# A written order for in-projection, attention and both feed-forward products of a Strassen-Winograd transformer layer

## The chip, the cores and the metric

The kernel runs on one core of one Trainium2 chip. What counts is the device time of one execution in microseconds, as the median of several runs. A profile is one execution taken by the hardware profiler. A core has five engines that run their own queues of instructions: TensorE (PE, with its weight loads shown as PEld), VectorE (DVE), ScalarE (ACT), GpSimd (POOL) and SyncE (SP). SP, ACT and POOL also issue DMA transfers.

## The reference, cut to what matters

One layer, S = 512 tokens, D = 2048, DFF = 8192, eight attention heads of 128, all in float32:

```python
h = rmsnorm(x, g_mix[l])
z = jnp.einsum('bsd,dc->bsc', h, w_in[l])
cb, cc, cv, q, k, v, f_logit, gate_c, gate_a = jnp.split(z, SPLIT_POINTS, axis=-1)
conv_branch = jnp.einsum('bsc,cd->bsd', cb * causal_dwconv(cc * cv, conv_w[l]), w_conv_out[l])
log_f = jax.nn.log_sigmoid(f_logit + b_f[l])
attn = forgetting_attention(q, k, v, log_f)     # softmax(q k / sqrt(d) + c_q - c_k, causal) v, c = cumsum(log_f)
attn_branch = jnp.einsum('bsc,cd->bsd', attn, w_attn_out[l])
mixed = sigmoid(gate_c + b_c) * conv_branch + sigmoid(gate_a + b_a) * attn_branch
x = x + jnp.einsum('bsd,de->bse', mixed, w_mix_out[l])
h2 = rmsnorm(x, g_mlp[l])
u = jnp.square(jnp.maximum(jnp.einsum('bsd,df->bsf', h2, w_ff1[l]), 0.0))
x = x + jnp.einsum('bsf,fd->bsd', u, w_ff2[l])
return rmsnorm(x, g_final)
```

The lines are shortened; the gates, the merge and the squared ReLU are written as one line each.

## The kernel before, in words

**Products.** The in-projection, ff1 and ff2 are cut into 2 x 2 blocks, and each such block product is done by Strassen-Winograd with seven products instead of eight. They are named by their operand on the side of the tokens: A11, A12, A22 and the sums S1 to S4. On the side of the weights stand four quarters X00, X01, X10 and X11, each of 1 MB, 128 x 2048, and sums of them that DVE makes in place (`sub`, L104). Before TensorE can use a quarter it is split: ACT copies it to a rounded high half (`th`, L100), DVE subtracts that to get the low half (`tl`, L101). A product is then three passes, high by high, high by low and low by high. In the in-projection and ff1 (`mm_cols`, L142, L144, L146) a product is 48 matmuls of width 256; the low half is used only by the last 16. In the V groups and ff2 (`mm_rows`, L159, L161, L164) it is 24 matmuls of width 512 (narrower in V). `th` and `tl` have two buffers each, the quarters four (x0 to x3), and results in flight (`o`) five.

**Groups.** A `Group` holds the seven products of one set of columns. `head` runs A11 and A12, `tail` the other five in the order S4, S2, S3, S1, A22; between them stand the sums of the quarters and the evictions of the accumulators a to d, one PSUM bank each. The stages in order of time: RMSNorm and transposes of x; heads of five groups (V and four of k and q), their tails; the second V group; six groups for the conv's inputs (z) and, ahead of the first four of them in the text, the eight calls of `attend(h)`; then eight groups for the gates; the outputs of conv and attention (`gemm_t`); the mix product (`gemm_n`); sixteen groups of ff1; ff2 in eight segments of two units of seven products; the final norm and the output.

**Attention.** For each head and each block of 128 query rows, TensorE makes the scores (L547 to L549), DVE the maximum (L551), ACT the exponential (L557), DVE scales, TensorE transposes (L563), DVE copies (L565), TensorE multiplies with v (L567). k, q and v of a head come back from DRAM (kq_d, v_d) over SP's queue.

**What sets the order.** The text gives every instruction, but the framework's scheduler decides where it stands on its engine, so a piece of attention lands wherever it fits between or inside products. In z and gates, groups n = 4, 7, 10 and 13 have a matmul of width 192 into an unused bank in the middle of S4 (`apart`), and so has every third group of ff1. All loads of weights and nearly all stores and reloads of intermediate results are issued by SP. The feed-forward's sums for ff2 (`s_d`, L858 and L859) go out by POOL through one buffer `r`, and are loaded again as `us` (L908) by POOL.

**ff2.** Each unit loads four weight quarters (y, L973), runs A11, S3, S2, A22, S1, A12, S4 and adds its accumulators unscaled to the result of 128 x 1024 at a time (`into`, L107). In the last segment the row factor `turned`, the residual and the gain of the last norm are applied (`finish`, L941 and L944; `residual`).

## Time and profile before

| | us |
|---|---|
| three runs | 2488.52, 2493.36, 2494.16 (median 2493.36) |
| the profiled execution | 2488.25 |
| its span in the trace | 2486.4 |
| start of the first and of the last group of matmuls | 6.5 and 2472.2 |
| attention and its 28 products | 272 to 492 |
| rest of z, and gates | 492 to about 870 |
| ff1 | about 1230 to 1855 |
| ff2 | 1856 to 2474 |

The page gives for every engine its busy time and share of the span, then the span in slices. A row of a window gives start:end, its length, then busy time and count of instructions for each engine, the clock granted to TensorE (1.00 is full), the share of the DMA engines and the rate in GB/s. A row of waits reads: the waiting engine, what it would write, its line, an arrow, the engine and line that released it, and then total us, how often, and the longest. A row of the timeline or of the chain begins with start and duration.

### The profile page before, as it was taken

The numbers are of one execution on the slowest core, as the hardware profiler recorded it, in microseconds if no ns is written. First come the engines' busy times: TensorE is split into PE (matmuls) and PEld (weight loads), VectorE is DVE, ScalarE is ACT, GpSimd is POOL, SyncE is SP. The second block draws the span as 40 slices with busy tenths as digits, with TensorE's granted clock in tenths as the row PEclk, the third lists the DMA queues.
The fourth block names the chain that finished last, engine by engine and source line by source line (L and its number), as shares of the span: only waits on it lengthen the run. The fifth ranks groups of instructions, "written<-read, shape, count | busy, mean of one in ns | idle before, by whom it ended". The sixth has DMA issues, their size and how long they took to land.

```text
span 2486.4 us, 39025 instructions
## 1 busy us (share of the span) xinstructions
PE 2436.8 (98%) x16910; PEld 2250.5 (91%) x16910; DVE 1898.7 (76%) x1498; ACT 1146.3 (46%) x1136; POOL 112.3 (5%) x184
## 2 busy tenths in 40 slices
PE   8999999999999999999999999999999999999997
PEld 7999999999999988888889999999998888888885
DVE  7877676789777743425688898888987888878888
ACT  5433443344544622225556666656665333333344
POOL 0000000000000000000000000000011000000010
PEclk9999999999999999999999999999999999999998
DMA  7555544456544554335645656556488566655573
GB/s 239 169 168 160 156 133 149 143 172 219 161 132 132 184 167 154 115 136 200 214 160 189 231 180 225 198 197 239 173 302 295 185 217 220 236 183 175 201 254 118
DMA packets 289920, 465.08 MB, mean 187 GB/s; under 512 B 10236, under 2 KB 194644, under 8 KB 289620
## 3 DMA queue, kind: packets, MB, share of 16 engines
q1 hardware_dynamic: 260704, 330.40, 41.6%
q0 software_dynamic: 28176, 131.08, 14.1%
q8 instruction: 133, 2.18, 0.4%
q10 hardware_dynamic: 868, 1.10, 0.1%
q14 instruction: 39, 0.32, 0.0%
HBM read 370.26 MB, written 92.27 MB: 186 GB/s over the span
## 4 chain that ended last, share of the span: by engine, by line
PE 68%; DVE 8%; DMA 4%; issue 2%; ACT 2%; SPq 0%; POOL 0%; POOLq 0%; DVEq 0%; ACTq 0%
PE pn L326 7%; PE pt L307 7%; PE a L142 5%; PE a L144 5%; PE a L146 4%; PE a L159 4%; PE a L164 4%; PE a L161 4%; DVE tl L101 3%; PE d L144 3%; PE d L142 3%; PE d L146 3%; PE d L159 2%; PE d L161 2%; PE d L164 2%; DMA x<-in_w_ff_dram 2%
## 5 line engine op out<-in xcount | busy, mean ns | idle before, releaser
L101 DVE TENSOR_TENSOR tl<-x,th 128x2048 fp32r<-128x2048 f32 (+1 forms) x252 | 574.9, 2287 | 208.3 <-ACT th L100 185.9
L100 ACT ACTIVATE th<-x 128x2048 fp32r<-128x2048 f32 (+1 forms) x252 | 482.4, 1917 | 507.7 <-PE a L144 170.5
L104 DVE TENSOR_TENSOR x<-x,x 128x2048 f32<-128x2048 f32 (+1 forms) x144 | 329.1, 2285 | 18.4 <-DMA x<-in_w_ff_dram 10.9
L100 ACT ACTIVATE th<-y 128x2048 fp32r<-128x2048 f32 x80 | 153.5, 1918 | 245.7 <-DVE y L104 92.4
L101 DVE TENSOR_TENSOR tl<-y,th 128x2048 fp32r<-128x2048 f32 x80 | 182.7, 2284 | 35.2 <-ACT th L100 35.2
L142 PE MATMUL a<-ST,th 128*128 128x256 f32 x768 | 179.6, 279 | 7.1 <-ACT th L100 7.1
L101 DVE TENSOR_TENSOR tl<-raw,th 128x2048 fp32r<-128x2048 f32 x40 | 91.6, 2290 | 121.2 <-ACT th L100 121.0
L144 PE MATMUL a<-ST,th 128*128 128x256 f32 x768 | 178.7, 278 | 0.0
L100 ACT ACTIVATE th<-raw 128x2048 fp32r<-128x2048 f32 x40 | 76.8, 1920 | 210.8 <-PE pt L307 107.3
L159 PE MATMUL a<-th,us 128*128 128x512 f32 x512 | 157.7, 389 | 1.5 <-ACT o L867 1.5
L161 PE MATMUL a<-th,us 128*128 128x512 f32 x512 | 157.6, 389 | 0.0
L142 PEld LDWEIGHTS a<-ST,th 128*128 128x128 f32 x768 | 145.4, 189 | 8.2 <-ACT th L100 7.9
L144 PEld LDWEIGHTS a<-ST,th 128*128 128x128 f32 x768 | 145.3, 189 | 0.0
L142 PE MATMUL a<-S,th 128*128 128x256 f32 x576 | 133.9, 278 | 4.1 <-ACT th L100 4.1
L326 PE MATMUL pn<-th,m 128*128 128x512 f32 x512 | 134.4, 391 | 0.0
L144 PE MATMUL a<-S,th 128*128 128x256 f32 x576 | 133.4, 277 | 0.0
L307 PE MATMUL pt<-act,th 128*128 128x512 f32 x512 | 126.6, 389 | 1.0 <-DVE o L107 1.0
L164 PE MATMUL a<-tl,us 128*128 128x512 f32 x512 | 126.4, 389 | 0.0
L142 PE MATMUL d<-ST,th 128*128 128x256 f32 x512 | 118.3, 277 | 0.0
L144 PE MATMUL d<-ST,th 128*128 128x256 f32 x512 | 118.2, 277 | 0.0
L159 PEld LDWEIGHTS a<-th,us 128*128 128x128 f32 x512 | 96.0, 188 | 21.6 <-ACT o L867 1.6
L307 PEld LDWEIGHTS pt<-act,th 128*128 128x128 f32 x512 | 96.0, 188 | 21.0 <-issue 1.2
(280 smaller groups left out, 5860.0 us busy)
## 6 DMA issues: line engine op xcount, KB each, us to landing
x<-in_w_in_dram SPq DMA_DIRECT2D x86, 1024.0 KB, 5.8
x<-in_w_ff_dram SPq DMA_DIRECT2D x66, 1024.0 KB, 8.3
y<-in_w_ff_dram SPq DMA_DIRECT2D x64, 1024.0 KB, 6.3
us<-s_d POOLq DMA_DIRECT2D x48, 1024.0 KB, 8.9
s_d<-rh POOLq DMA_DIRECT2D x32, 896.0 KB, 5.9
s_d<-r POOLq DMA_DIRECT2D x32, 896.0 KB, 8.0
raw<-in_w_mix_out_dram SPq DMA_DIRECT2D x24, 1024.0 KB, 5.1
g_d<-o SPq DMA_DIRECT2D x32, 256.0 KB, 2.2
```

Of the source, the lines that this page charges most:

```text
L100: nc.scalar.activation(out=hi, in_=src, func=AF.Copy)
L101: nc.vector.tensor_tensor(out=lo, in0=src, in1=hi.bitcast(F32), op=ALU.subtract)
L104: nc.vector.tensor_tensor(out=out, in0=a, in1=b, op=ALU.subtract)
L142: nc.tensor.matmul(o, hi[:, q, js], Sh, start=first and q == 0 and j == 0, stop=False, skip_group_check=True)
L144: nc.tensor.matmul(o, hi[:, q, js], Sl, start=False, stop=False, skip_group_check=True)
L146: nc.tensor.matmul(o, lo[:, q, js], Sh, start=False, stop=q == nq - 1, skip_group_check=True)
L159: nc.tensor.matmul(o, Sh[:, ts], hi[:, q, :], start=begin, stop=False, skip_group_check=True)
L161: nc.tensor.matmul(o, Sl[:, ts], hi[:, q, :], start=False, stop=False, skip_group_check=True)
L164: nc.tensor.matmul(o, Sh[:, ts], lo[:, q, :], start=False, stop=q == nq - 1, skip_group_check=True)
L307: nc.tensor.matmul(ps[j], w[:, q, j * P:(j + 1) * P], a, start=first, stop=last)
L326: nc.tensor.matmul(ps[t], A[t][e], w[:, q, :], start=first, stop=last)
```

## The change

The tails of the first five groups and everything up to the end of the gates, and then ff1, ff2 and the end, stand in blocks in which the scheduler is switched off (`with manual()`) for TensorE, DVE, ACT, POOL and SP: their queues hold the instructions in the order of the text. The rest (start, the five heads, conv and attention outputs, mix) is scheduled as before. The text of that order is written by a `Pipe`. Its step k emits, for product k: an attention piece if one is due, a sum, the split, another sum; then the eviction of product k-2, the store of product k-3, work postponed to this step; then the matmuls of product k-1:

```diff
+    class Pipe:
+        def step(self, p=None, sub=None, after=None, early=None, guest=False):
...
+            visit = self.visits.pop(0) if guest and self.visits else None
+            if visit:
+                p.high()
+                visit.first()
+            if sub:
+                sub()
+            if p:
+                p.split()
+            if visit:
+                visit.second()
+            if after:
+                after()
+            if last and not early:
+                last.evict()
+            if old:
+                old.finish()
+            for work in self.todo.pop(self.n, ()):
+                work()
+            if cur:
+                cur.go()
...
-            self.run(c, "S4", X[1, 1], True)
-            sub(X[0, 0], X[0, 1], X[0, 0])
-            sub(X[0, 1], X[1, 1], X[0, 1])
...
+            pipe.step(self.product("S4", (1, 1), "c", True), after=next(turns), guest=True)
+            p = self.product("S3", (0, 1), "d", True)
+            pipe.step(p, after=next(turns))
+            p = self.product("S2", (0, 0), "a", False)
+            pipe.step(p, after=next(turns), guest=True)
+            p = self.product("A22", (1, 0), "d", False)
+            pipe.step(p, after=next(turns), guest=True)
+            p = self.product("S1", (1, 1), "a", False)
+            pipe.step(p, guest=True)
```

The pipe isn't emptied at the end of a group: the first products of the next group follow in the same steps, and each quarter of the next group is loaded as soon as one of this group's buffers comes free. The order within a group is now A11, A12, S4, S3, S2, A22, S1.

**Attention** is 24 pieces: per head rows 0 and 1 together, row 2, row 3. A visit stands at the start of a product, in five of the seven products of a group: TensorE does the output of the piece before last, the transposes of the last one and the scores of the new one, and then the product. With two visits for the forget sums and two to run out they fill the 28 products of the first groups of z. The convolutions stand in the first four groups of gates, and the reload and split of the conv's and attention's results in the last one. The fetch of the next head's k, q and v is issued by POOL in the visit that reads the last row of the head before:

```diff
+        def first():
+            if a:
+                a.out()
+            if b:
+                b.turned()
+            if c:
+                c.scores(i)
+            if b:
+                b.kept()
+            if c:
+                c.weigh()
+            if a and a.at[-1][0] == NT - 1:
+                a.stored()
+            if c and c.at[-1][0] == NT - 1 and i + 1 < len(rows):
+                rows[i + 1].fetch()
```

On TensorE, in the attention, stood before (th and tl are the halves of weights, S_885 a sum of tokens, o, tp and sc the attention's output, transposes and scores):

```order
L146 MATMUL a<-S_885,tl 128x256 x2
L567 MATMUL o<-pt,vv 128x128 x3
L146 MATMUL a<-S_885,tl 128x256
L563 MATMUL tp<-ident,p 128x128 x4
L146 MATMUL a<-S_885,tl 128x256 x8
L567 MATMUL o<-pt,vv 128x128 x4
L146 MATMUL a<-S_885,tl 128x256 x5
```

and stands now, at the border of two products:

```order
L150 MATMUL a<-A_146,tl 128x256 x16
L737 MATMUL o<-pt,vv 128x128 x3
L726 MATMUL tp<-ident,p 128x128 x3
L699 MATMUL sc<-kT,qT 128x512
L700 LDWEIGHTS sel
L700 MATMUL sc<-cparts,sel 128x512
L701 LDWEIGHTS identb
L701 MATMUL sc<-maskb,identb 128x128
L146 MATMUL b<-A_147,th 128x256
```

The pieces of attention have moved from inside a product to its end, three kinds together.

**Stores and fetches** of v, k and q, z, gates, attention and conv results go from SP's queue to POOL's (`nc.sync.dma_start` becomes `nc.gpsimd.dma_start`), so that SP issues in these stages the loads of weights alone. POOL's queue in the attention now reads (none of these stood there before):

```order
L690 DMA kT<-kq_d 128x512
L690 DMA qT<-kq_d 128x512
L692 DMA vv<-v_d 128x4x128
L773 DMA z_d<-o 128x2x256 x2
L690 DMA kT<-kq_d 128x512
L690 DMA qT<-kq_d 128x512
L692 DMA vv<-v_d 128x4x128
```

A fetch of a head and the stores of z share one queue here. The four dummy matmuls of z and gates are removed; those of ff1 stay.

**ff1's start.** All four quarters of the first group are loaded first. The transposes of the last columns of tokens (`Q2.turn(1, 3)`) stand inside A11's matmuls, the mean over rows comes only after S4 is issued, S4 takes the token chunks of the last column at its end (`late`), and of that column's sums the low halves of S2 and S1 are postponed:

```diff
+    with manual():
+        g0 = groups[0]
+        for ij in ((0, 0), (1, 0), (1, 1), (0, 1)):
+            g0.load(*ij)
+        g0.begin(True, True)
+        squares_of_rows()
+        Q2.gained(1, 3)
+        behind = []
+        Q2.sums(3, behind)
...
+        g0.rest(groups[1], at)
+        chain(groups[1:], units[0], lambda n: load_sums(0, LOADS.index(n)) if n in LOADS else None)
+        for unit, ahead in zip(units, units[1:]):
+            unit.run(ahead, during(unit))
+        units[-1].close()
```

**ff2.** The order of a unit is A11, A12, S2, S3, S1, A22, S4, and in the last unit A11, S3, S2, A22, S1, A12, S4, with S4's matmuls by blocks of rows, one block to its end and then the other. Each eviction is a scaled addition of 128 x 512 (`turned`, L1238) per bank, so the row factor is applied from the start; residuals are added in segments 1 to 4, the gain of the last norm four or eight steps after the last eviction. The sums of a unit's weights are made partly one unit ahead, which needs X11 of the next unit in the buffer that the S4 of this one frees. DVE before, across a change of unit (y are quarters, t a sum, x the result):

```order
L101 TENSOR_TENSOR tl<-y_19170,th 128x2048
L101 TENSOR_TENSOR tl<-y_19395,th 128x2048
L104 TENSOR_TENSOR y_19395<-y_19397,y_19395 128x2048
L104 TENSOR_TENSOR y_19397<-y_19399,y_19397 128x2048
L107 TENSOR_TENSOR x_18493<-a,x_18493 128x2x512
L104 TENSOR_TENSOR t_19462<-y_19399,y_19395 128x2048
L101 TENSOR_TENSOR tl<-y_19397,th 128x2048
```

and now, where the second row is the low half of S4 and y_19598 is the next unit's X11, loaded into the buffer of y_19365:

```order
L106 TENSOR_TENSOR t_18429<-y_19500,y_19400 128x2048
L106 TENSOR_TENSOR tl<-y_19365,th 128x2048
L1238 SCALAR_TENSOR_TENSOR x_18428<-a,turned,x_18428 128x512 x2
L106 TENSOR_TENSOR tl<-y_19400,th 128x2048
L1238 SCALAR_TENSOR_TENSOR x_18428<-d,turned,x_18428 128x512 x2
L106 TENSOR_TENSOR t_18429<-y_19598,t_18429 128x2048
L106 TENSOR_TENSOR tl<-y_19502,th 128x2048
L1238 SCALAR_TENSOR_TENSOR x_18427<-a,turned,x_18427 128x512 x2
```

Between the release of the buffer and the first reader of the new quarter stand two evictions and one low half. The loads of `us` are split by products (A11 and A12; S2 and S3; S1 and A22; S4) and issued by POOL as soon as the products of the segment before that read the same place are done. At the end, a row's output is two transfers of 512 KB, one by ACT and one by SP.

More of the change, by code (lines that the diff above doesn't have):

```diff
@@ L211, in snap, with plus @@
             return s
-        def plus(self, s, ps, scale=1.0):
+        def plus(self, s, which, scale=1.0):
+            ps = self.A[which]
             if len(ps) == 1:
@@ L639, in tile_hybrid_block, with acted @@
+    seq = heads + [gV1] + zs + gates
+    with manual():
+        for g, after in zip(seq, seq[1:] + [None]):
+            if "a" not in g.A:
+                g.begin(True)
+            g.rest(after, during(g))
+        take(2)
+        pipe.end()
+        pipe.drain()
+    def acted(*tags):
+        return lambda k: tuple(e[:, k % 4, :] for e in acts[tags[k // 4]])
+    yact, aact = acted(0, 1), acted(2, 3)
     ph.close()
```

922 lines of the change are left out of this document (557 added, 365 removed).

## The prediction

> **What bounds the kernel now.** I read the page first, for the engine that is full.
>
> ```profile
> span 2486.4 us, 39025 instructions
> PE 2436.8 (98%) x16910; PEld 2250.5 (91%) x16910; DVE 1898.7 (76%) x1498; ACT 1146.3 (46%) x1136; POOL 112.3 (5%) x184
> PE   8999999999999999999999999999999999999997
> ```
>
> TensorE is busy in 98% of the span, and the change leaves its matmuls as they are (four dummies fewer). So it can only win the time in which TensorE stands, starts cold or runs below its pace. The table of windows, asked by stage, shows where that is (columns: window, length, busy time of PE, PEld, DVE, ACT, POOL, granted clock, DMA share, GB/s).
>
> ```profile
> 75.00:245.00 170.00, 163.98 (x1417) 162.79 (x1416) 134.63 (x75) 65.91 (x48) 3.79 (x4) 1.00 0.52 164
> 272.00:492.10 220.10, 217.26 (x1726) 201.49 (x1725) 160.08 (x236) 88.85 (x122) 0.10 (x1) 1.00 0.45 142
> 1225.00:1375.00 150.00, 141.69 (x1189) 139.79 (x1187) 121.25 (x95) 83.35 (x88) 7.72 (x13) 0.99 0.54 178
> 1288.00:1298.00 10.00, 7.26 (x51) 7.06 (x50) 10.00 (x7) 6.31 (x5) 1.15 (x2) 0.83 0.45 184
> 1375.00:1850.00 475.00, 474.78 (x4172) 474.35 (x4171) 415.12 (x310) 299.94 (x299) 28.19 (x52) 1.00 0.60 212
> 1900.00:2430.00 530.00, 530.00 (x2340) 438.85 (x2339) 440.74 (x248) 193.20 (x114) 44.54 (x60) 1.00 0.64 213
> 2438.00:2444.00 6.00, 4.29 (x12) 3.45 (x13) 6.00 (x4) 3.57 (x2) 0.00 (x0) 0.72 0.01 3
> 2474.00:2486.40 12.40, 0.15 (x1) 0.00 (x0) 4.16 (x9) 4.65 (x9) 1.10 (x2) 0.62 0.87 328
> ```
>
> Steady ff1 and steady ff2 (1375 to 1850, 1900 to 2430) have nothing to win: TensorE never stops, at 113.9 ns per 256-wide matmul (475/4172) and 226.5 ns per 512-wide one. The losses are at the seams: tails of the heads, attention, the start of ff1, the last ff2 unit, the end. What TensorE waits for there, from the view of waits by window (total, times, longest):
>
> ```profile
> PE a L142 <- ACT th L100: 3.6, 4, 1.4
> PE a L159 <- ACT th L100: 1.5, 1, 1.5
> PE c L159 <- ACT th L100: 0.9, 1, 0.9
> ...
> PE sc L547 <- DMA qT<-kq_d: 2.4, 3, 1.0
> ...
> PE a L142 <- ACT th L100: 6.9, 3, 2.7
> PE c L142 <- ACT th L100: 1.4, 1, 1.4
> ...
> PE pt L307 <- DVE o L107: 1.0, 1, 1.0
> PE a L159 <- ACT o L867: 1.5, 1, 1.5
> PE d L159 <- ACT th L100: 4.6, 1, 4.6
> ```
>
> The first three are the tails (6.0 us), the fourth attention, the next two the start of ff1 (8.3 us), the last three the start of the conv output, the start of ff2 and its last unit. Nearly always the high half (th, ACT) of a product comes late, although ACT is 46% busy: it waits itself for a sum on DVE. The order of DVE's queue decides, and that is what the change rewrites.
>
> A second loss is pace. Three runs of 16 equal matmuls in the chain: in the attention stage, in the gates and at the start of ff1.
>
> ```profile
> 430.85 1.89 PE a L146 x16
> ...
> 551.14 1.81 PE a L146 x16
> ...
> 1339.39 1.88 PE a L146 x16
> ```
>
> That is 118, 113 and 118 ns, 5.67 or 5.43 us per product of 48. In the records a stretch keeps one pace for many products and changes it at an interruption; an attention piece often leaves the slow one behind.
>
> **The change part by part.** Each gain is what a stage loses now, less what I expect to stay.
>
> Attention. 28 products at 5.44 us are 152.3 us of the stage's 220.1. The prices of its pieces are distances in the timeline and one run of the chain:
>
> ```profile
> 383.44 0.38 PE L547 MATMUL sc<-kT,qT 128*128 128x128 f32 x2
> 384.40 0.36 PE L142 MATMUL a<-A,th 128*128 128x256 f32 x1
> 392.19 1.13 PE L547 MATMUL sc<-kT,qT 128*128 128x512 f32 x2
> 393.40 0.36 PE L142 MATMUL b<-A,th 128*128 128x256 f32 x1
> 425.12 1.02 PE o L567 x8
> ```
>
> Scores of two short rows together, or of row 2, take 0.96 us (384.40 - 383.44; I take the same for row 2), of row 3 1.21: 8 x 3.13 = 25.0 us. The 160 output matmuls and 80 transposes of width 128 lie between 0.113 us (a 256-wide one) and 1.02/8 = 0.127: 27 to 30.5. With 1 to 3 for the forget sums (eight small instructions, where 1.21 pays three), 53 to 58.5 us; so 9 to 15 are lost now to slow pace, restarts and waits. Afterwards a product is interrupted once, at its start, and not at several places inside. I leave 4 to 5 (slow pace after half of 28 visits 0.24 x 14 = 3.4, the fetch of qT 0 to 2): **gain 7**, bounds 0 and 12.
>
> The fetch is the new exposed step. kT and qT of the next head may be issued only when row 3's scores have read the old ones; the next scores come after one product (5.44) and about 1 us of output and transposes: some 6.5 us. Their landings before, and the issue time of a POOL transfer (longer ones, hence an upper end):
>
> ```profile
> kT<-kq_d SPq DMA_DIRECT2D x8, 256.0 KB, 6.0
> qT<-kq_d SPq DMA_DIRECT2D x8, 256.0 KB, 3.2
> L908 POOL DMA_DIRECT2D us<-s_d x64: 748/748/770, 1830.4 to 2392.6; - x64
> ```
>
> Two issues (1.5) and 3.2 to 6.0 make 4.7 to 7.5: nothing to 1 us at each head change, seven times, fewer where the visit pattern leaves two products between. That is the 0 to 2 above, at worst 7. Stores moved from SP to POOL cost TensorE nothing: they sit behind an eviction, and no matmul waits for them; gone from SP, they no longer hold up weight loads behind an SP wait.
>
> Here a page speaks against the change. Row L908: 64 issues of POOL take 748 to 770 ns while DVE is busy in 83% of the window (440.74/530), so nothing shows POOL being shut out. The Trainium skill, "DMA: Bandwidth & Descriptors", section "SWDGE vs HWDGE vs iDMA", says that descriptor rings of POOL-issued transfers are SBUF state from which DVE locks GpSimd out in its 2-port mode, and that transfers issued from SP or ACT are immune. By that rule the moved fetches would be late; it is a rival below.
>
> Tails of V and kq. 6.0 us of waits. The pipe emits the split of product k while k-1 runs, and sums one product ahead: **gain 5.5**, 0 to 6.
>
> Start of the conv output and of ff2: waits of 1.0 and 1.5. The first goes because the reload and split of y and a is spread over the last gate group, the second because ff2's first sums are loaded and split in the same pipe: **gain 1.2 each**, 0 to 1.5.
>
> Start of ff1. 8.3 us of waits, 10 us at a clock of 0.83 behind the longest (1.7), and seven products at slow pace (1.7): 11.7. The chain shows why: a weight quarter arrives late, and sums and splits queue behind it.
>
> ```profile
> 1270.74 7.88 DMA x<-in_w_ff_dram
> 1278.64 2.29 DVE x L104
> ```
>
> Afterwards all four quarters are loaded ahead, the sums of the last column are cut into two urgent and two postponed low halves, and S4 takes that column's chunks last: **gain 10**, 5 to 11.7.
>
> Last ff2 unit. A wait of 4.6, then 6 us at 0.72 (1.7): DVE is busy for the whole of that window and just before it, with finishing passes of the unit before queued ahead of this unit's sums. Afterwards the sums are made a product ahead and the gain passes are postponed by four to eight steps: **gain 5.3**, 2 to 6.3. End: 12.4 us follow the last matmul. S4 by row blocks closes one half early and each row leaves in two larger transfers; the last eviction, mean, scaling and transfer stay: **gain 2**, 0 to 4.
>
> ff2's steady state is where the change can cost. Evictions become one scaled pass per bank; DVE's prices in the chain of waits, and the landings of weight loads (y, from the source view: min, median, max):
>
> ```profile
> 2425.93 1.40 DVE x L941 x2
> 2427.33 2.20 DVE tl L101
> 2435.45 2.21 DVE y L104
> DMA to landing us min/median/max: 6.0/6.3/11.4
> ```
>
> Per unit 7 low halves and 4 sums at 2.2 and 12 evictions at 0.7: 32.6 us (33.8 with a residual, half the elements of a sum and so about 1.2) of 7 x 5.44 = 38.1. It fits, at 86 to 89%. But in written order DVE stops at whatever is late. The next unit's X11 can be loaded only into the buffer that S4's low half releases, about when TensorE ends S1. Its first reader stands behind the eviction of A22: 5.44 + 1.40 = 6.9 us later, and about 1 more passes before TensorE notices. So up to 7.9 us (6.7 with the residual) cost nothing; 6.3 is free; the high end, 11.4, is 3.5 too late. At the 7 changes of segment a pair of us loads is in flight when X11 is issued; the middle of 6.3 and 11.4, about 9, costs there (9 - 7.9) x 7 = 8, plus 1.2 for four residuals = 12 at most. I take **loss 5**, 0 to 17.
>
> Steady ff1. A chain through the single r buffer is written out too. Its DVE work is as before (415.12 of 475), it has about 2 us to spare per group, and the store's landing lies within it (row of L859):
>
> ```profile
> DMA to landing us min/median/max: 3.8/8.0/10.0
> ```
>
> **Loss 1**, 0 to 5.
>
> The sum: 7 + 5.5 + 1.2 + 1.2 + 10 + 5.3 + 2 = 32.2 gained, 6 lost, 26.2 net. The profiled execution took 2488.25 us in all, so 2462. The median of the three runs, 2493.36, lies 5.1 above that execution, which is below the lowest of them (2488.52); I add about half: **2464 us**. Gains and losses at their better ends (44 and 0) would give 2446; with attention 4, ff1's start 4 and ff2 6 worse, 2478: that is the case's own range.
>
> **Rivals.**
> *Slow pace stays* (0.22). Four dummy matmuls are gone from z and gates, where the row of 551.14 shows the fast pace. If the last visit leaves the slow pace, the rest of z and eight groups of gates, some 58 products, run at 5.67: 58 x 0.24 = 14 us, 2478. For it: the row of 430.85. Against it: the pace changes at interruptions, and the last visits (outputs and transposes without scores) and every short wait are further ones that can bring the fast one back.
>
> *DVE locks out POOL* (0.05). Each fetch of kT and qT waits for a DVE pass, up to 2.2 us each, at up to seven head changes: half of 7 x 4.4 = 15 us, 2479; row L908 speaks against it.
>
> *The X11 loop decides, and it gets slower* (0.08). If X11 lands at 11.4 us at all 15 changes of unit, 15 x 3.5 + 8 x 1.2 = 62 us are lost instead of 5: 2521. It eats the whole gain of about 31 from a mean landing near 9.5 us on ((9.5 - 7.9) x 15 + 9.6 = 34). For it: the single slot and the maximum 11.4. Against it: the median 6.3, and us loads fall on half of the changes.
>
> *The written order does not deliver in attention* (0.07). A visit's DVE work is bound to scores on TensorE:
>
> ```profile
> L565 DVE COPY pt<-tp 128x128 f32<-128x128 f32 (+3 forms) x32 | 15.7, 489 | 19.2 <-PE tp L563 19.1
> L551 DVE TENSOR_REDUCE nm<-sc 128x1 f32<-128x128 f32 (+3 forms) x32 | 15.1, 482 | 10.2 <-PE sc L549 9.7
> ```
>
> Copy 0.5, maximum 0.5 to 0.7, low half 2.2, scaling about 0.4, one sum 2.2, eviction 0.7: 6.6 of the 5.44 + 1.9 = 7.3 us of a step. If ACT's exponential in the middle costs 1.5 more, every one of 28 steps is late by 0.8: 22 us, 2486 to 2490.
>
> *All at their better ends* (0.08): 2444 to 2450.
>
> **How the numbers follow.** Forecast 0.50, slow pace 0.22, lock 0.05, X11 0.08, attention 0.07, better 0.08. Low 2445, high 2487: outside are X11, half of attention and some of the better end, about 0.15. A measurement of this kernel tells about 0.2% from no change, 5 us. Faster (under 2488.4): 0.50 + 0.22 + 0.05 + 0.08 + a part of attention = 0.87; the same 0.05; slower 0.08, the X11 case.
>
> **What would show it.** Right: no wait above 1 us at the start of ff1 nor in the last unit, granted clock 1.00 there; the time between the first and last score near 213 us instead of 220; 256-wide runs of 16 in the gates at 1.81. Wrong: gates at 1.89; waits of TensorE for th in ff2, with DVE idle until y lands, at each unit's A12 or S2; waits of sc for qT above 1 us at every head; POOL issues longer than 0.77 us. If steady ff2 needs more than 38.2 us per unit, the forecast falls by its own term.

## The result and the profile after

The changed kernel takes 2464.26 us (median of 4 runs, 2461.30 to 2467.21), the kernel before 2491.64 (4 runs, 2488.52 to 2494.16). The ratio is 0.9891, with a 95% interval of 0.9873 to 0.9908. The profiled execution of the changed kernel took 2464.56, which is 23.7 less than that of before. The forecast for it was 2462, and 2464 for the median. The median was met within 1 us, the profiled execution within 3. The stages below show that this is partly luck: the gains in attention, ff1 and the tails were forecast too low, and the loss in ff2 was forecast at about a third of what it was.

The page of the changed kernel (span; busy time by engine; TensorE and its granted clock in 40 slices):

```profile
span 2462.8 us, 39037 instructions
PE 2429.9 (99%) x16906; PEld 2243.7 (91%) x16906; DVE 1914.6 (78%) x1557; ACT 1147.0 (47%) x1140; POOL 214.7 (9%) x343
PE   7999999999999999999999999999999999999998
PEclk9999999999999999999999999999999999999999
```

TensorE now is busy in 99% of a shorter span. The last slice of the clock, an 8 in the kernel before, is a 9 now. POOL's busy time doubled, since it issues the stores and fetches.

To compare the stages I cut both traces at the same events: first product of the tails, first product of z, first matmul of the conv output, first product of ff1, first matmul of ff2, last matmul, end. The table of windows of before, cut there (the second number is a stage's length):

```profile
0.00:87.40 87.40, 74.08 (x610) 73.07 (x610) 68.57 (x80) 48.58 (x60) 7.12 (x17) 0.98 0.73 230
87.40:272.00 184.60, 179.49 (x1541) 178.50 (x1542) 138.68 (x79) 73.02 (x56) 0.00 (x0) 1.00 0.52 163
272.00:875.30 603.30, 599.00 (x5091) 582.86 (x5089) 462.83 (x440) 276.33 (x309) 0.81 (x8) 1.00 0.50 156
875.30:1230.10 354.80, 354.80 (x1593) 294.13 (x1594) 162.78 (x173) 121.27 (x158) 11.06 (x15) 1.00 0.49 165
1230.10:1858.20 628.10, 618.11 (x5394) 616.49 (x5393) 540.20 (x409) 385.87 (x391) 39.12 (x70) 1.00 0.59 206
1858.20:2473.80 615.60, 610.99 (x2688) 505.43 (x2688) 521.28 (x314) 236.38 (x157) 53.05 (x73) 1.00 0.62 208
2473.80:2486.40 12.60, 0.35 (x2) 0.00 (x0) 4.36 (x10) 4.85 (x10) 1.10 (x2) 0.63 0.87 330
```

The same of the changed kernel:

```profile
0.00:88.80 88.80, 75.52 (x610) 74.57 (x611) 68.67 (x80) 48.53 (x60) 9.73 (x21) 0.98 0.71 226
88.80:266.80 178.00, 178.00 (x1543) 178.00 (x1542) 134.70 (x75) 72.34 (x54) 13.08 (x18) 1.00 0.54 170
266.80:857.80 591.00, 590.88 (x5087) 578.55 (x5085) 463.31 (x425) 270.71 (x302) 86.21 (x143) 1.00 0.50 158
857.80:1213.10 355.30, 355.08 (x1593) 294.00 (x1593) 169.41 (x180) 125.54 (x166) 13.13 (x18) 1.00 0.50 168
1213.10:1828.20 615.10, 612.99 (x5394) 612.36 (x5394) 541.18 (x405) 386.38 (x386) 38.53 (x69) 1.00 0.59 203
1828.20:2452.50 624.30, 617.02 (x2690) 506.28 (x2689) 533.70 (x388) 240.53 (x171) 52.96 (x73) 0.99 0.62 213
2452.50:2462.80 10.30, 0.38 (x2) 0.00 (x0) 3.58 (x8) 2.97 (x5) 1.10 (x2) 0.63 0.51 205
```

The count of matmuls in a row is the same within four, so each pair of rows holds the same work. The lengths give:

| stage | before | after | won | forecast |
|---|---|---|---|---|
| start and heads | 87.4 | 88.8 | -1.4 | 0 |
| tails of V and kq, second V group | 184.6 | 178.0 | 6.6 | 5.5 |
| z with attention, gates | 603.3 | 591.0 | 12.3 | 8.2 |
| conv and attention outputs, mix | 354.8 | 355.3 | -0.5 | 0 |
| ff1 | 628.1 | 615.1 | 13.0 | 10.2 |
| ff2 | 615.6 | 624.3 | -8.7 | 0.3 |
| after the last matmul | 12.6 | 10.3 | 2.3 | 2 |
| span | 2486.4 | 2462.8 | 23.6 | 26.2 |

(The waits before the conv output and before ff2 end at the cuts, so in the forecast's column the first 1.2 stands with z, and the second with ff1, beside the 10 and the loss of 1. ff2 has the last unit's 5.3 and the loss of 5.) ff2 got slower where I had it about even. What TensorE still waits for from the tails on, in the changed kernel's view of waits:

```profile
PE a L164 <- DVE x L1238: 4.0, 1, 4.0
PE a L164 <- ACT th L245: 3.0, 2, 2.8
...
PE d L139 <- ACT th L245: 0.8, 1, 0.8
PE a L146 <- ACT o L288: 0.7, 1, 0.7
PE a L150 <- DVE tl L106: 0.6, 1, 0.6
```

The first two rows are ff2 (L164 is its first pass), the other three the start of ff1. The waits for th in the tails are gone, and so are all waits for qT. The two in ff2 also cost the clock, as the windows around them show:

```profile
1860.00:1872.00 12.00, 8.04 (x23) 5.88 (x22) 10.52 (x8) 1.40 (x1) 0.00 (x0) 0.72 0.71 234
1922.00:1930.00 8.00, 5.07 (x15) 3.49 (x15) 8.00 (x6) 1.91 (x1) 0.00 (x0) 0.79 0.46 163
```

In the first, 12 us hold 23 matmuls of 0.2265 us, or 5.2 us of work: 6.8 us are lost, 4.0 by the wait and 2.8 by the clock at 0.72. In the second 8.0 - 15 x 0.2265 = 4.6 us are lost, 2.8 of them by a wait for a high half. DVE's timeline at the first shows how it came about:

```profile
1851.61 2.28 DVE L106 TENSOR_TENSOR tl<-t,th 128x2048 fp32r<-128x2048 f32 x1
1859.95 2.29 DVE L106 TENSOR_TENSOR t<-y,y 128x2048 f32<-128x2048 f32 x1 [6.06 <-DMA y<-in_w_ff_dram]
1862.16 2.28 DVE L106 TENSOR_TENSOR tl<-y,th 128x2048 fp32r<-128x2048 f32 x1
1864.36 1.40 DVE L1238 SCALAR_TENSOR_TENSOR x<-a,turned,x 128x512 f32<-128x512 f32 x2
```

DVE stands 6.06 us before the sum for the next unit, whose quarter is late. Behind that sum in its queue lie a low half and the eviction of S1. TensorE needs the bank of S1 for S4. It had finished what precedes S4 at about 1861 and goes on at 1865.20, when the first half of the eviction is done. The sum itself wasn't urgent; the eviction was.

### The profile page after: what moved, and what is told of

The parts are those of the page before. It is cut to its first block, busy times and chain, and to the rows that moved or that the text cites. A ratio compares the mean times of both kernels' runs of the same rounds, so it can differ in the third digit from the quotient of the medians.

```text
span 2462.8 us, 39037 instructions
## 1 busy us (share of the span) xinstructions
PE 2429.9 (99%) x16906; PEld 2243.7 (91%) x16906; DVE 1914.6 (78%) x1557; ACT 1147.0 (47%) x1140; POOL 214.7 (9%) x343
## 4 chain that ended last, share of the span: by engine, by line
PE 93%; DVE 3%; issue 2%; ACT 1%; DMA 1%; POOL 0%; ACTq 0%; POOLq 0%; DVEq 0%
PE a L146 7%; PE a L148 7%; PE a L150 7%; PE pn L465 7%; PE pt L446 7%; PE a L164 5%; PE d L146 5%; PE a L166 5%; PE d L148 5%; PE d L150 5%; PE a L169 5%; PE b L146 2%; PE d L166 2%; PE d L164 2%; PE b L148 2%; PE c L146 2%
## 5 line engine op out<-in xcount | busy, mean ns | idle before, releaser
L106 DVE TENSOR_TENSOR x<-x,x 128x2048 f32<-128x2048 f32 (+1 forms) x108 | 246.8, 2286 | 2.8 <-DMA x<-in_w_ff_dram 2.7
L245 ACT ACTIVATE th<-y 128x2048 fp32r<-128x2048 f32 x66 | 126.8, 1922 | 208.6 <-PE a L166 107.0
L164 PE MATMUL a<-th,us 128*128 128x512 f32 x512 | 163.2, 397 | 7.3 <-DVE x L1238 4.0
L245 ACT ACTIVATE th<-t 128x2048 fp32r<-128x2048 f32 x46 | 88.2, 1918 | 156.2 <-PE a L166 97.0
L106 DVE TENSOR_TENSOR tl<-y,th 128x2048 fp32r<-128x2048 f32 x66 | 150.9, 2286 | 12.9 <-ACT th L245 12.9
L166 PE MATMUL a<-th,us 128*128 128x512 f32 x512 | 160.7, 394 | 0.0
L106 DVE TENSOR_TENSOR tl<-t,th 128x2048 fp32r<-128x2048 f32 x46 | 105.3, 2290 | 51.6 <-ACT th L245 51.6
L164 PEld LDWEIGHTS a<-th,us 128*128 128x128 f32 x512 | 97.6, 191 | 32.3 <-issue 4.9
L146 PE MATMUL d<-ST,th 128*128 128x256 f32 x512 | 117.8, 276 | 0.0
```

Source lines behind the costliest of these rows:

```text
L106: nc.vector.tensor_tensor(out=out, in0=a, in1=b, op=ALU.subtract)
L146: nc.tensor.matmul(o, hi[:, q, js], Sh, start=first and q == 0 and j == 0, stop=False, skip_group_check=True)
L164: nc.tensor.matmul(o, Sh[:, ts], hi[:, q, :], start=begin, stop=False, skip_group_check=True)
L166: nc.tensor.matmul(o, Sl[:, ts], hi[:, q, :], start=False, stop=False, skip_group_check=True)
L245: nc.scalar.activation(out=self.hi, in_=self.src, func=AF.Copy)
```

## The experiments

**Two losses in ff2, one edit each.** The first edit moves the broadcast of the last norm's gain (gf). In the changed kernel it is issued at the end of segment 0, and it landed late (row of its source line: min, median, max):

```profile
DMA to landing us min/median/max: 13.3/13.3/13.3
```

```diff
-        nc.gpsimd.dma_start(out=late["gf"], in_=g_final.partition_broadcast(P))
+    def fetch_gain():
+        nc.gpsimd.dma_start(out=late["gf"], in_=g_final.partition_broadcast(P))
...
+            if n == "S2" and (seg, cg) == (5, 0):
+                fetch_gain()
```

> The changed kernel with one edit: the broadcast of the last norm's gain (gf) is issued in segment 5 and not at the end of segment 0. Theory A, a transfer in the way: gf (13.3 us to land) delays X11 of the third ff2 unit, which landed after 12.1 us; without it X11 lands in 6 to 9 us, the 3.0 us wait of TensorE at about 1922 and the 2 us of cold clock behind it go, and the profiled execution falls from 2464.6 to about 2460. Rival B, the pairs of us loads alone delay X11: it still takes 10 us or more, the wait stays, 2464.

Measured: 2457.99 us (one run, span 2456.3). ff2 took 619.0 us from its first to its last matmul, and not 624.3. X11 of the third unit landed after 6.39 us instead of 12.1, and from 1900 to 2400 TensorE ran without a stop, 499.90 us of 500 for 2201 matmuls. Theory A holds for the second loss: the broadcast was in the way. In segment 5 gf itself took 12.6 us, and nobody waited for it.

The second edit evicts S1 first in the first unit:

```diff
                       self.minus(u[:, 1], ahead.X[0, 1], ahead.X[0, 0]),
+                      early=(lambda p: None) if self.u is None else None)
```

> The changed kernel with one edit: in the first ff2 unit alone DVE evicts S1 before, not after, the sum for the next unit and the low half of S4. Theory A, an in-order queue: DVE stood 6.1 us before a sum whose quarter was late, and the eviction for which TensorE waited was queued behind it; with the eviction ahead, the wait of 4.0 us at about 1861 and 3.2 us of cold clock go, 2464.6 to about 2457.5. Rival B, the late quarter itself is needed: the low half of S4 then comes late in its place, 2 to 4 us of wait stay, 2460 to 2463.

Measured: 2464.22 us (one run), no change. The view of waits, 1850 to 1935, tells why:

```profile
PE a L164 <- DVE x L1238: 4.8, 1, 4.8
PE a L164 <- ACT th L245: 2.3, 1, 2.3
PE a L166 <- DMA us<-s_d: 1.4, 1, 1.4
```

The first wait did go. 1.4 us remained of it, now for the loads of us. But a wait of 4.8 us for an eviction now stands at 1900, at the S4 of the second unit, with a cold clock behind it. The same queue order is in every unit, and the quarter that the second unit's sum reads came late too: it landed after 15.0 us. Neither theory had it: the gain was given back one unit later, because the fault was in the rule and the edit mended one place of it.

Both edits:

```diff
+    def fetch_gain():
...
+                      early=(lambda p: None) if self.u is None else None)
```

> Both edits together, gf in segment 5 and S1 evicted first in the first unit. Theory A: the two losses are separate and add, 12 us, about 2452.5 profiled; ratio to the kernel before about 0.984. Rival B: removing the first stall brings TensorE earlier to the second, and only the larger one is won, 2457 to 2460.

Measured: median 2462.27 (4 runs, 2459.55 to 2465.96), ratio 0.9876 (0.9855 to 0.9897). Theory A was wrong, and B's value was too good: the second unit's wait stayed (5.0 us for the eviction), so of the two gains only that of gf is there (ff2 620.8 us), and the interval doesn't tell it from the changed kernel.

The next variant asks for X11 earlier, by putting the sum behind the low half of S4:

```diff
             pipe.step(self.product("S4", X[1, 1], "a", False, (0, 1, True)),
-                      self.minus(u[:, 1], ahead.X[0, 1], ahead.X[0, 0]),
+                      after=self.minus(u[:, 1], ahead.X[0, 1], ahead.X[0, 0]),
                       early=(lambda p: None) if self.u is None else None)
```

> As e3, and in every unit the sum X01 - X00 of the next unit stands behind the low half of S4 instead of ahead of it, so that X11 of the next unit is asked for one DVE pass (2.2 us) earlier. If the X11 loop has its slack in the steady state (my sum: a landing up to 7.9 us is free, and 6.1 to 6.3 was measured there), the time is that of e3 within 1 us, and only DVE's waits for y shrink (22.8 us in 12 places). If the loop is at its limit, 2 to 5 us are won over e3.

Measured: median 2463.98 (4 runs), ratio 0.9880 (0.9864 to 0.9897). DVE's waits for y fell from 22.8 to 3.0 us, and the time didn't fall. No long wait is left in ff2, but the units from the second to the fourteenth lose 0.65 to 0.71 us each at S4 (38.73 to 38.79 us a unit; the kernel before takes 38.08). Rows of DVE and of TensorE around one of them:

```profile
1935.31 2.29 DVE L106 TENSOR_TENSOR tl<-y,th 128x2048 fp32r<-128x2048 f32 x1 [0.70 <-ACT th L245]
1937.52 2.29 DVE L106 TENSOR_TENSOR t<-y,y 128x2048 f32<-128x2048 f32 x1
1939.72 1.40 DVE L1240 SCALAR_TENSOR_TENSOR x<-a,turned,x 128x512 f32<-128x512 f32 x2
```

```profile
1940.56 1.11 PE L164 MATMUL a<-th,us 128*128 128x512 f32 x2
1941.51 0.62 PE L166 MATMUL a<-th,us 128*128 128x512 f32 x2
```

The eviction of S1 starts at 1939.72 and takes 0.7 us per bank. TensorE could have begun S4 a little earlier and follows it bank by bank. Here the low half starts only when ACT's high half is there, and the eviction still comes last. So the eviction is what must not stand behind the sum. Hence the version that mends the rule, with gf in segment 5 and in each unit low half, eviction, sum:

```diff
             if last and not early:
                 last.evict()
+            if behind:
+                behind()
...
             pipe.step(self.product("S4", X[1, 1], "a", False, (0, 1, True)),
-                      self.minus(u[:, 1], ahead.X[0, 1], ahead.X[0, 0]))
+                      behind=self.minus(u[:, 1], ahead.X[0, 1], ahead.X[0, 0]))
```

> The changed kernel with gf in segment 5, and in every ff2 unit's step of S4 the order low half of S4, eviction of S1, sum X01 - X00 for the next unit (as it is: the sum first, the eviction last). Theory A: the eviction for which TensorE waits is no longer behind a sum that may stand before a late quarter, nor behind 4.4 us of passes, and X11 is asked for 2.2 us earlier; the wait of 4 to 5 us with its cold clock near 1861 goes and does not come back one unit later, and the hitch of 0.65 us per unit of the variant with the eviction last does not appear: steady ff2 38.1 us per unit, profiled about 2451, 6 us below the one with gf late alone. Rival B: the quarters at the start of ff2 are late in themselves (12 us beside the stores of ff1 and the us loads) and the first wait only moves to the next reader: 2456 to 2460.

Measured: median 2456.39 (5 runs, 2451.65 to 2457.09), ratio to the kernel before 0.9849 (0.9827 to 0.9872). It beats both kernels: its highest run lies below the lowest of the changed kernel. TensorE's only wait from 1840 to 1940, DVE's waits for y in all of ff2, and the steady units:

```profile
PE a L166 <- DMA us<-s_d: 1.5, 1, 1.5
```

```profile
DVE t L106 <- DMA y<-in_w_ff_dram: 4.0, 3, 1.8
```

```profile
1870.00:2400.00 530.00, 529.86 (x2337) 438.35 (x2336) 457.65 (x325) 198.47 (x120) 48.99 (x67) 1.00 0.65 221
```

The mechanism is as theory A had it: no wait for an eviction, none one unit later, no hitch in the steady units (38.08 us each from the second to the fourteenth). From its first to its last matmul ff2 takes 614.4 us, against 624.3 in the changed kernel and 615.6 before: the order and the place of gf were the whole loss. The profiled time of 2457.09 lies in rival B's numbers all the same. This execution lost some 3 us more at the start of the conv output and 2 more in the last two units than the changed kernel's, and I didn't follow these up.

**The written order itself.** The scheduler is left on, over the same text:

```diff
     def manual():
-        E = mybir.EngineType
-        return tc.manual_schedule(engines={E.PE, E.DVE, E.Activation, E.Pool, E.SP})
+        return nullcontext()
```

> The changed kernel's text with the scheduler left on: the blocks that keep the written order are taken away, the pipe's code, its pieces, its queues and its product order stay. Theory A, the written order is the gain: the scheduler puts attention pieces inside products again and queues sums ahead of urgent splits, and at least half of the 27 us is lost, 2476 to 2495. Rival B, the restructured text is the gain (products a step ahead, loads into freed buffers): 2460 to 2468.

Measured: median 2578.74 (4 runs), ratio to before 1.0347 (1.0322 to 1.0372): 114 us slower than with the order written, and 87 slower than the kernel before. That is theory A's direction, far beyond its numbers, but not its mechanism: in the two traces TensorE's matmuls stand in the same order up to the start of ff1, attention pieces included, and in all but 45 of 16906 places in the whole. What the scheduler orders otherwise are the queues of DVE, ACT and POOL. The largest waits of TensorE in its trace:

```profile
PE d L146 <- ACT o L288: 28.1, 14, 3.1
PE b L150 <- DVE tl L106: 16.4, 11, 2.7
PE d L164 <- DVE x L1238: 11.2, 6, 2.8
```

They are waits for evictions (o, x) and low halves that the scheduler put too late; 25.0 of the first row's 28.1 us lie in ff1. Attention, 260 to 575, had no wait at all, and lost no more than with the order written. The tails took 177.8 us (89.6 to 267.4), as with the order written (178.0) and not as before (184.6). In these two stages the new text carries the gain (pieces of attention three kinds together between products, splits a product ahead; its parts weren't told apart). The written order isn't needed for it there.

With the scheduler on in the in-projection and attention alone:

```diff
-    with manual():
+    with nullcontext():
         for g, after in zip(seq, seq[1:] + [None]):
```

> The changed kernel with the scheduler left on in the in-projection and attention alone; ff1, ff2 and the end stay in the written order. With everything scheduled it took 2579, and the trace put most of the loss in ff1 and ff2. Theory A, by that trace: 10 to 15 us slower than the changed kernel, 2474 to 2480, lost in the gates with the convolutions (575 to 675), not in attention. Rival B, attention loses too once the queues behind it are in order: 2485 or more.

Measured: median 2477.43 (10 runs, 2473.84 to 2486.88), ratio 0.9943 (0.9924 to 0.9962). Theory A holds: 13 us of the 114 belong to this half, lost not in attention but in the gates with the convolutions, where waits of 10.5 us stand between 575 and 700. (The runs fall into two groups, 11 and 20 us above the changed kernel; a second loss in the upper one follows below.) All matmuls stand in the written order here. One wait of that part matters for what follows, at about 649:

```profile
PE b L150 <- DVE tl L106: 2.6, 1, 2.6
```

**No end of a group.** The pipe is emptied at each border of groups:

```diff
             g.rest(after, during(g))
+            pipe.end()
...
             g.rest(*((after,) if after else (ahead, hook)))
+            if after:
+                pipe.end()
```

> The changed kernel with the pipe emptied at the end of each group (in-projection and ff1, 35 borders), else the same. Theory A: at each border TensorE waits for the high half of the next group's A11, since a split is then only emitted when the last product has been issued: ACT's pass of 1.9 us behind evictions, 1 to 3 us each, 2500 to 2570. Rival B: ACT and DVE run ahead over the border anyway since nothing in the queue waits, 2464 to 2475.

Measured: 2675.30 us (one run), 211 more than the changed kernel. In its view of waits:

```profile
PE a L146 <- ACT th L245: 123.9, 28, 5.8
```

That is 4.4 us at each of 28 borders, more than the 1 to 3 of theory A, and the time lies above its range. Sums, low half and high half all follow the border in this text; which of them makes up the difference wasn't told apart. The page's granted clock is below full in several slices of ff1. This says what a border would cost in this pipe. It is no part of the gain over the kernel before, where the scheduler ran over the borders anyway.

**The queues.** All stores, fetches and reloads of in-projection and attention on SP again (ten places in the text):

```diff
-                nc.gpsimd.dma_start(out=made[name], in_=kq_d[k, self.h])
+                nc.sync.dma_start(out=made[name], in_=kq_d[k, self.h])
...
-            nc.gpsimd.dma_start(out=z_d[g // 2, f:f + 2, :, i * HS:(i + 1) * HS].rearrange("b p c -> p b c"), in_=v)
+            nc.sync.dma_start(out=z_d[g // 2, f:f + 2, :, i * HS:(i + 1) * HS].rearrange("b p c -> p b c"), in_=v)
```

> The changed kernel with all stores, fetches and reloads of the in-projection and attention issued by SP again and not by POOL, order as written. Theory A, SP's queue in written order stands before a store until its eviction is done, and weight loads behind it start late: TensorE waits for th in the tails and in z, 10 us or more slower, 2475 or more. Rival B, buffers come free late enough that the loads lose nothing: 2462 to 2467. By the rule on DVE and POOL's descriptors it would be faster instead, by up to 5 us.

Measured: median 2461.52 (4 runs, 2459.75 to 2466.70), ratio 0.9882 (0.9858 to 0.9907), against 0.9891 (0.9873 to 0.9908): no difference. Rival B holds. The move to POOL is no part of the gain. The other way round, the kernel before with the same transfers on POOL:

```diff
-            nc.sync.dma_start(out=z_d[g // 2, f:f + 2, :, i * HS:(i + 1) * HS].rearrange("b p c -> p b c"), in_=v)
+            nc.gpsimd.dma_start(out=z_d[g // 2, f:f + 2, :, i * HS:(i + 1) * HS].rearrange("b p c -> p b c"), in_=v)
```

> The kernel before, with only these stores, fetches and reloads moved from SP to POOL, still scheduled. Theory A: the move by itself is worth little where the scheduler orders both queues, within 3 us of the kernel before; the qT waits (2.4 us) may go. Rival B: the queue is a large part of the gain, 5 to 10 us faster.

Measured: median 2501.25 (10 runs, 2499.03 to 2505.09), ratio 1.0041 (1.0029 to 1.0052). Both theories missed: it is 10 us slower. The wait for qT doubled:

```profile
PE sc L547 <- DMA qT<-kq_d: 5.0, 4, 2.5
```

Those are 2.6 of the 12.0 us by which the profiled span is longer. Others are stops of 3.3 us in sum at 616 to 633 in the gates, 2.4 at the start of the span, and 3.6 of slow pace in ff1. Why the scheduled kernel loses there and the written one doesn't was not tried further.

**The start of ff1.** Two of its measures undone:

```diff
-                     extra={"A11": lambda q, *_: Q2.turn(1, 3) if q == KT // 2 - 1 else None, "S4": (None, 2), "S3": "first"}
+                     extra={"A11": lambda q, *_: Q2.turn(1, 3) if q == KT // 2 - 1 else None, "S3": "first"}
...
-        Q2.sums(3, behind)
+        Q2.sums(3)
```

> The changed kernel, in the first group of ff1 without two of its measures: S4 takes the token chunks in their order (the last column not at the end), and the low halves of the last column's S2 and S1 are made at once and not after S4 is issued. Theory A, these two carry the gain of 10 to 13 us at the start of ff1: 5 us or more come back as waits of TensorE for th or ST near 1230. Rival B, the early loads and the sums made one product ahead carry it: 0 to 2 us.

Measured: median 2462.36 (4 runs, 2460.30 to 2462.78), ratio 0.9876 (0.9852 to 0.9901). The waits at the start of ff1 are 0.7 and 0.6 us, no more than the 2.1 of the changed kernel. Rival B holds: the late chunks and the postponed low halves carry nothing. The quarters loaded ahead, the sums made a product ahead and the transposes inside A11 remain as the cause; which of the three wasn't told apart.

**The dummies and the pace.** The kernel before without the four dummies of z and gates:

```diff
                     whole(Group(w_in, g * S, g * S + HS, HS, Q1.moving, mm_cols, steady(n), put_z,
-                    extra=apart(4) if n == NH // 2 else {}))
+                    extra={}))
...
-                    extra=apart(4) if f % 6 == 2 else {}))
+                    extra={}))
```

> The kernel before without the four dummy matmuls of width 192 in z and gates. Theory A, a dummy sets the fast pace: without them the products after attention run at 118 ns per matmul, 5.66 against 5.44 us, for 40 to 70 products: 9 to 15 us slower. Rival B, interruptions of any kind set the pace, as the changed kernel's gates at 5.44 without dummies suggest: within 3 us of the kernel before.

Measured: median 2495.76 of ten runs, ratio 1.0022 (1.0000 to 1.0045). The median hides that the ten fall into two groups: five from 2484.03 to 2492.53, five from 2499.00 to 2505.15, means 2488.7 and 2502.9. They lie 14.2 us apart, which is what 59 to 68 products at the slow pace would cost (0.24 or 0.21 us each), but the profiled execution (2487.12) is of the lower group, and its gates run at the fast pace. So neither theory is shown by its trace. The kernel before, dummies in place, has runs of the upper height too: four of the 21 measured beside it, 2499.56 to 2501.52. The slow pace itself is in a trace of the variant with the in-projection scheduled. Its ten runs, too, fall into two groups (six from 2473.84 to 2478.38, four from 2482.04 to 2486.88), and its profiled execution, 2486.88, is of the upper one. Here are 210 us of gates in that trace, in the changed kernel's, and in that of the variant with everything scheduled:

```profile
660.00:870.00 210.00, 210.00 (x1785) 210.00 (x1784) 149.90 (x91) 106.81 (x113) 20.71 (x31) 1.00 0.46 145
```

```profile
620.00:830.00 210.00, 210.00 (x1855) 210.00 (x1854) 167.45 (x112) 103.39 (x107) 30.10 (x52) 1.00 0.52 165
```

```profile
660.00:870.00 210.00, 210.00 (x1856) 210.00 (x1855) 155.81 (x98) 109.70 (x120) 20.67 (x31) 1.00 0.49 153
```

TensorE is busy throughout in all three, at the full clock and with the same kind of matmul: 117.6 ns per matmul in the first, 113.2 and 113.1 in the others. The slow pace began at the wait of 2.6 us quoted above and held for 40 products to the end of the gates: 40 x 0.21 = 8.4 us, beside 9.1 between the groups' means (2484.5 and 2475.4). No execution of the lower group was profiled, so that the pace makes the two groups fits the numbers but isn't shown. The wait alone doesn't set the pace either. In the third trace the matmuls stand in the same order, a wait of 2.7 us stands at the same place, the mean clock of the 8 us from 650 on is the same (0.79), and the fast pace follows.

## Why the prediction came out right, step by step

**Attention and z** ("gain 7", with the conv's start 8.2) won 12.3. The mechanism was right, the gain too small: I had left 4 to 5 us of loss, and hardly any is left. Of the 591.0 us of this row the 98 products take 533.1 at 5.44; the other 57.9 lie inside the 53 to 58.5 that I had priced for the pieces. There is no wait for qT (the forecast's 0 to 2), and a product without a visit beside one with a visit took mostly 5.53 to 5.55 us, 0.1 above the fast ones, where I had charged 0.24 to half of 28. The fetch came out at the short end, its issues and landings (from the source view of the fetches):

```profile
L690 POOL DMA_DIRECT2D kT<-kq_d x8: 557/568/582, 274.0 to 495.2; - x8
L690 POOL DMA_DIRECT2D qT<-kq_d x8: 544/548/557, 274.6 to 495.8; - x8
...
DMA to landing us min/median/max: 2.7/3.1/4.6
```

With 1.1 us for two issues and a landing of 3.1 to 4.6, qT is there 4 to 6 us after the scores have read the old one, inside the 6.5 that I had worked out. I had priced an issue by a longer one (0.75).

One sign that I named can't be read as I wrote it. I had put 28 visits into 28 products, as the description of the change does. But a visit stands in five of seven products, so the visits reach over about 40 products of z. From the first to the last score it is 231 us now and 186 before, neither 213 nor 220. The sum doesn't rest on this, since it counts visits.

**The rival of the lock** is refuted for this kernel. POOL's issues took 544 to 582 ns, nearly constant, through the attention stage where DVE works most of the time, and the fetches on SP give the same time. The sign that I had named, issues above 0.77 us, came up in four of POOL's 313 (0.79 to 0.92 us). By the Trainium skill, "DMA: Bandwidth & Descriptors", section "SWDGE vs HWDGE vs iDMA", POOL-issued transfers are open to interference from DVE. No run here shows it. The 10 us of the kernel before with its transfers on POOL aren't evidence for it either, since qT landed there after 2.9 to 5.1 us.

**Tails** (5.5) won 6.6, a little above the bound of 6, and the waits are gone, as stated. The start and the heads, forecast unchanged, lost 1.4; in the profiles of variants with the same text up to there the first product of the tails begins between 87.0 and 90.2.

**ff1** (10 at its start, a loss of 1 in the steady groups, 1.2 before ff2: 10.2) won 13.0. The first 28 products won 9.1 of the 10; waits of 2.1 us are left of 8.3. The wait of 1.5 before ff2 is gone. The steady groups, where I had charged 1, won 2.4 instead: mostly, slow pace that the kernel before has in some products after 1500 doesn't appear, which I hadn't forecast and which is luck. The reason that I gave for the gain was half wrong: the postponed low halves and late chunks do nothing.

**ff2** failed: 0.3 faster was forecast, and it is 8.7 slower. The step that failed is "loss 5", put at the seven changes of segment; it measured 14.1. In the kernel before a unit takes 38.1 us. In the changed kernel the first takes 45.6, the third 43.1, and the twelve from the fourth on 38.1 to 38.5, together 1.6 too long; five of them are above the 38.2 that I had named as a sign.

The mechanism was right: a late quarter holds up DVE and, behind it, TensorE. The place was wrong. X11 landed after 6.1 to 6.3 us at fourteen of the fifteen changes of unit, where it is asked for ahead of the pair of us loads, and the landings of 9 to 15 us fell on quarters that had time in the steady state. Where X11 was late (12.1 us), in the third unit, it was because of gf. gf isn't new: the kernel before issues it by POOL at the same time, 1896.7, and there it landed after 4.8 us and not 13.3. I hadn't looked at what would be in flight beside it. My price for such a lateness, (12.1 - 7.9) = 4.2 us, is near the 4.6 lost, but by luck: the wait was 2.8 us, and the rest is the clock, which the price left out.

The larger loss, 6.8 us in the first unit, was another step of DVE's queue, the sum with the next unit's X01, which stands ahead of an eviction. I had only followed X11. The experiment with the order mended shows that both lie in the order and in the place of gf, not in the work: steady ff2 is then as before. The last unit gained its 5.3: its wait of 4.6 is gone.

**The end** won 2.3 of 2 forecast.

**The rival of the slow pace** didn't come up in the changed kernel: in its profile and those of its variants with the order written (but for the drained one, whose gates are full of stops) the gates run at 113 ns. What it describes does happen, as the variant with the in-projection scheduled shows: 118 ns for the 40 products until the stage's end, with no dummy to end it. What started it there isn't known.

**The rival of attention's order** was wrong: no wait of TensorE in that stage. **The X11 loop** as a cause of a slower kernel was wrong in size: it was late once in fifteen changes. (A slip in the range: the better ends of my gains add up to 43 and not 44, which puts that end at 2447.)

The total came out because errors cancelled: attention and ff1 won 6.9 us more than forecast (25.3 against 18.4) and tails and end 1.4 more, while ff2 gave 9.0 less and start and mix 1.9 less, in sum 2.6 less than the 26.2. That the median came closer still is luck too: I had added 2 us because the profiled execution of before was a low one, and that of the changed kernel was not.

## What to carry to other kernels

When a queue is put in a written order, ask of each instruction that can wait for a transfer what stands behind it, and put evictions for which TensorE waits ahead of sums for the next unit. Mend such an order as a rule and not at the place where it shows: mended in one unit, the loss came back in the next. And before crediting an order, a queue or a measure at a start, undo it alone: here the move to another DMA queue and two of the start's measures were worth nothing, and the gains of tails and attention stayed with the scheduler on. The order was worth 114 us over the same text scheduled, in the gates, ff1 and ff2, with TensorE's own order all but the same: the order on the other engines made it.

## What the runs showed of the hardware

TensorE ran 256-wide matmuls at the full granted clock at two paces, 113 and 118 ns, and kept the slow one for up to 40 products. Which pace follows an interruption can differ: in the two variants above with the same order of matmuls in the gates, a wait of 2.6 us was followed by the slow one, a wait of 2.7 us at the same place by the fast one. What sets it stays open.

The clock fell after some waits and not after others. Windows around a wait of 2.3 us (the variant with S1 evicted first), of 1.5 us (the mended order) and of 3.0 us (the variant with the in-projection scheduled, in ff2's third unit):

```profile
1922.00:1930.00 8.00, 5.60 (x18) 3.99 (x17) 8.00 (x6) 1.91 (x1) 0.00 (x0) 0.79 0.12 46
```

```profile
1862.00:1872.00 10.00, 8.54 (x38) 6.68 (x37) 7.76 (x6) 4.59 (x4) 0.00 (x0) 1.00 1.00 342
```

```profile
1945.00:1955.00 10.00, 6.86 (x29) 5.12 (x29) 9.86 (x6) 2.66 (x2) 0.00 (x0) 1.00 0.55 182
```

The first brought the clock to 0.79, the other two left it full. The Trainium skill, "TensorE: Matmul & The Clock Gate", section "HAM oscillation — how this bites in real kernels", puts the limit for idle gaps at about 3.4 us. Here 2.3 was enough, and the measurement decides. Since 3.0 us did nothing elsewhere, the length of such a wait alone doesn't decide; what else does isn't shown. The waits of 4.0 and 4.8 us quoted above both brought the clock down (0.72 and 0.82 over the 12 us around them).
